# Every weight product of a two-layer encoder with the activation stationary, and the operands that TensorE turns for it

## The chip, the core and the metric

The kernel runs on one core of one Trainium2 chip. The metric is device time in microseconds (us), the median of the runs. The core has five engines that work side by side and wait for each other by semaphores: TensorE (PE; its loads of the stationary operand are listed as PEld), VectorE (DVE), ScalarE (ACT), GpSimd (POOL) and SyncE (SP), on whose queue all transfers are issued here.

## The reference

Two layers of an encoder over 256 tokens with 2048 features, all in float32: an input projection, eight attention heads beside a gated position-mixing branch, an output projection, and a gated feed-forward part.

```python
D_MODEL = 2048; SEQ = 256; DEPTH = 2; D_ATTN = D_GMLP = 1024; N_HEADS = 8; D_FF = 5632
...
    for l in range(DEPTH):
        h = rmsnorm(x, norm1_g[l])
        proj = jnp.einsum('bsd,de->bse', h, w_in[l])
        q = proj[..., 0:D_ATTN].reshape(B, S, N_HEADS, HEAD_DIM)
        k = proj[..., D_ATTN:2 * D_ATTN].reshape(B, S, N_HEADS, HEAD_DIM)
        v = proj[..., 2 * D_ATTN:3 * D_ATTN].reshape(B, S, N_HEADS, HEAD_DIM)
        uv = proj[..., 3 * D_ATTN:]
        q = apply_rope(q, cos, sin)
        k = apply_rope(k, cos, sin)
        a = dilated_attention(q, k, v)
        g = chunked_spatial_gating(uv, gmlp_ln_g[l], w_spatial[l], b_spatial[l])
        mix = jnp.concatenate([rmsnorm(a, mix_norm_attn_g[l]),
                               rmsnorm(g, mix_norm_gmlp_g[l])], axis=-1)
        x = x + jnp.einsum('bse,ed->bsd', mix, w_out[l])
        h = rmsnorm(x, norm2_g[l])
        ff = jax.nn.silu(jnp.einsum('bsd,df->bsf', h, w_gate[l])) * jnp.einsum('bsd,df->bsf', h, w_up[l])
        x = x + jnp.einsum('bsf,fd->bsd', ff, w_down[l])
    return rmsnorm(x, final_g)
```

The three windows of the attention lie within 256 tokens, so the kernel computes them as one attention with the logarithm of the count of patterns in its mask (`mskt`).

## The kernel before

Each float32 operand is written as the sum of a high part, rounded to the type that TensorE reads at full pace (float32r), and a low part; a product is made of three terms: high by high, high by low, low by high (`TERMS`). ACT writes the high part (`hi`, L731), DVE the low part (`lo`, L732). Weights are read once, in the order of their use, by loads of 1 MB on SP's queue (`raw`, four buffers); a load brings two chunks of [128, 1024], and each chunk is split into `hi` and `lo` (four buffers each). The loop over chunks (from L749) issues the load three loads ahead, the split three chunks ahead (`LA_SPLIT`), then the chunk's products, then at most two side tasks (`run_side`). This order is written out by the program, engine by engine, and each engine executes its own list in order.

A weight product has one of two forms. In the form "tok" (L776) the activation is stationary, [128 features, 128 tokens], and 512 weight columns stream: three matmuls of 512 columns for each k-tile (128 input features) and token tile. The result is [token, feature]. v, the gating branch and, in the last layer, the down projection have it. In the form "feat" (L784) a [128, 128] tile of the weights is stationary and the activation streams: the high part of the weights meets high and low part of the activation side by side (512 columns), the low part meets the high part (256 columns):

```python
                            ps[:, t, :SEQ if wl else 2 * SEQ], lhsT=wt[wl][:, j, t * P:(t + 1) * P],
                            rhs=a.t[:, ka, 0, :] if wl else a.t[:, ka].rearrange("p a t -> p (a t)"),
```

The result is [feature, token], which is the layout that the next product wants (`KTiles`: the activation as [feature, token], high and low part). q, k, w_out, gate, up and the down projection of layer 0 have it. The two halves of such a result (by the high and by the low part of the activation) are added at the eviction (`add_halves` L525, `Ffn.scaled` L536), and the norm's factor for each token is multiplied in from a row that is broadcast over partitions by a matmul (`to_row`, L220, from sums over features, L208). x is held as [feature, token] and turned to [token, feature] by TensorE once, before the last projection (`Ffn.turn`, L572), since the output is [token, feature] (`Final`).

Of the kernel before, what the change touches and what calls it, by code (L numbers as in the profile page):

```python
# [8 lines left out]
F32 = mybir.dt.float32  # L9
# [29 lines left out]
CH = 1024  # L39
KCH = {"tok": 2, "feat": 4}  # L40
LA_DMA = 3
LA_SPLIT = 3
START = 2
WARM = 4
TAIL = 3
TERMS = ((0, 0), (0, 1), (1, 0))
# w_in: (what, form, column, index); q and k by two heads, the others by halves
W_IN = tuple(
    [("v", "tok", 2 * DA + i * NB, i) for i in range(2)]
    + [(what, "feat", c + m * 2 * P, m) for m in range(NH // 2) for what, c in (("q", 0), ("k", DA))]  # L50
    + [("gv", "tok", 3 * DA + DG + i * NB, i) for i in range(2)]
    + [("u", "tok", 3 * DA + i * NB, i) for i in range(2)]
# [3 lines left out]
def _units():  # L56
    """The weight products in their order: (layer, weight, form, first row, k-tiles, first column, what, index)."""
    for l in range(DEPTH):
        for what, form, col, idx in W_IN:
            yield l, "w_in", form, 0, KD, col, what, idx  # L60
        for what, row, kt in (("oa", 0, NH), ("og", DA, NG)):
            for m in range(KD // 2):
                yield l, "w_out", "feat", row, kt, m * 2 * P, what, m
        j0 = 0
        for i, nj in enumerate(FF_PARTS):
            for m in range(2 * j0, 2 * (j0 + nj)):
                yield l, "w_gate", "feat", 0, KD, m * 2 * P, "gate", m
                yield l, "w_up", "feat", 0, KD, m * 2 * P, "up", m
            form, width = ("feat", 2 * P) if l + 1 < DEPTH else ("tok", NB)
            for m in range(D // width):  # L70
                yield l, "w_down", form, j0 * NB, nj * KR, m * width, f"down{i}", m
            j0 += nj
# [3 lines left out]
def encoder_kernel(ctx: ExitStack, tc: tile.TileContext, x, w, ws, lng, cols, fg, cs, msk, out):  # L76
# [36 lines left out]
    def load_x(k0, k1):  # L113
        b = k0 // KR
        nc.sync.dma_start(out=xt[b][:, k0 - b * KR:k1 - b * KR, :], in_=x[:, k0:k1, :])
# [747 lines left out]
```

## Time and profile before

| what | us |
|---|---|
| median of 3 runs | 2180.19 |
| lowest and highest | 2180.03 and 2181.32 |
| span of the profiled execution (first to last instruction) | 2178.5 |
| median less that span: what lies around the instructions | 1.7 |
| PE busy in the span | 2160.7 |
| DVE busy | 1431.8 |
| ACT busy | 981.7 |

The rows below come from the profiled execution and are measured against its span; the runs were timed apart. A busy PE is one with a matmul somewhere in its pipeline, so the pace of a kind of matmul is read from the distance of their starts, or from a long stretch with their number, and not from the duration of one. The granted clock of TensorE was at its full level in all 40 slices of the span.

### The profile page before, as it was taken

How to read it: one execution, taken by the hardware profiler on the slowest of the kernel's cores; microseconds unless marked ns; L12 is line 12 of the kernel's file. 1: busy time of each engine (PE TensorE's matmuls, PEld its weight loads, DVE VectorE, ACT ScalarE, POOL GpSimd, SP SyncE). 2: the span in 40 equal slices, each digit the busy share in tenths (PEclk: the TensorE clock that was granted, in tenths of full speed). 3: DMA queues.
4: the chain of work that ended last, by engine and by line, in shares of the span. 5: the costliest groups of instructions: out<-in, count | busy, mean ns of one | idle time of the engine just before them, and what ended most of it. 6: DMA issues, size and time to landing. Idle time of an engine off the chain costs nothing.

```text
span 2178.5 us, 28345 instructions
## 1 busy us (share of the span) xinstructions
PE 2160.7 (99%) x11692; PEld 1857.0 (85%) x11692; DVE 1431.8 (66%) x1515; ACT 981.7 (45%) x1192; POOL 120.4 (6%) x78
## 2 busy tenths in 40 slices
PE   8999999999999999999999999999999999999998
PEld 7888888888888888888888888888888888888886
DVE  6786677666556665566658866876665566645665
ACT  6455555443334443344545554554443344433443
POOL 2220002000000000000102200110000000000000
PEclk9999999999999999999999999999999999999999
DMA  7445555545554455554554455545455545555453
GB/s 289 167 155 193 181 187 186 182 175 200 186 193 179 176 201 179 193 186 177 199 187 162 156 191 183 184 176 192 185 184 193 186 180 193 193 193 193 180 207 116
DMA packets 57585, 404.01 MB, mean 185 GB/s; under 512 B 6512, under 2 KB 6512, under 8 KB 9456
## 3 DMA queue, kind: packets, MB, share of 16 engines
q1 hardware_dynamic: 57456, 402.21, 50.8%
q8 instruction: 91, 1.49, 0.3%
q14 instruction: 38, 0.31, 0.0%
HBM read 400.09 MB, written 2.10 MB: 185 GB/s over the span
## 4 chain that ended last, share of the span: by engine, by line
PE 94%; DVE 3%; ACT 2%; issue 0%; DMA 0%; SPq 0%; POOLq 0%; POOL 0%; DVEq 0%; ACTq 0%
PE mm L784 70%; PE mm L776 22%; ACT hi L731 1%; DVE lo L732 1%; DVE rb_k L339 1%; DVE rb_q L339 1%; ACT sm L386 0%; DVE pT L187 0%; PE op L409 0%; DVE mx L383 0%; PE mix L481 0%; DVE sm L378 0%; DMA raw<-in_w 0%; PE mm_end L776 0%; PE sp L373 0%
## 5 line engine op out<-in xcount | busy, mean ns | idle before, releaser
L732 DVE TENSOR_TENSOR lo<-raw,hi 128x1024 fp32r<-128x1024 f32 (+1 forms) x753 | 926.9, 1244 | 546.2 <-ACT hi L731 543.2
L784 PE MATMUL mm<-h_n,hi 128*128 128x512 f32 x3328 | 1165.6, 399 | 0.0
L731 ACT ACTIVATE hi<-raw 128x1024 fp32r<-128x1024 f32 (+1 forms) x753 | 784.2, 1054 | 626.2 <-PE mm L784 417.5
L784 PE MATMUL mm<-h_n,lo 128*128 128x256 f32 x3328 | 900.6, 281 | 0.0
L784 PEld LDWEIGHTS mm<-h_n,hi 128*128 128x128 f32 x3328 | 612.7, 188 | 133.6
L784 PEld LDWEIGHTS mm<-h_n,lo 128*128 128x128 f32 x3328 | 628.2, 189 | 20.0
L776 PE MATMUL mm<-hi,h_n 128*128 128x512 f32 x768 | 246.6, 396 | 4.6 <-ACT hi L731 4.6
L784 PE MATMUL mm<-ff,hi 128*128 128x512 f32 x704 | 245.0, 398 | 0.0
L776 PE MATMUL mm<-hi,ff 128*128 128x512 f32 x680 | 210.4, 389 | 0.0
L784 PE MATMUL mm<-ff,lo 128*128 128x256 f32 x704 | 189.8, 281 | 0.0
L776 PEld LDWEIGHTS mm<-hi,h_n 128*128 128x128 f32 x768 | 145.3, 189 | 34.9 <-ACT hi L731 4.9
L784 PEld LDWEIGHTS mm<-ff,hi 128*128 128x128 f32 x704 | 129.2, 188 | 27.9
L776 PE MATMUL mm<-lo,h_n 128*128 128x512 f32 x384 | 150.7, 392 | 0.0
L776 PEld LDWEIGHTS mm<-hi,ff 128*128 128x128 f32 x680 | 127.6, 188 | 26.5
L784 PEld LDWEIGHTS mm<-ff,lo 128*128 128x128 f32 x704 | 132.9, 189 | 4.7
L776 PE MATMUL mm<-lo,ff 128*128 128x512 f32 x340 | 132.3, 389 | 0.0
L179 ACT ACTIVATE ff<-up 128x512 fp32r<-128x512 f32 x44 | 27.8, 633 | 200.6 <-DVE up L553 200.6
L250 POOL TENSOR_TENSOR acc_n<-acc_n,sq_n 128x512 f32<-128x512 f32 x28 | 55.6, 1986 | 899.6 <-issue 688.4
L546 ACT ACTIVATE sil<-sil 128x512 f32<-128x512 f32 x44 | 27.9, 634 | 162.7 <-DVE sil L545 162.7
L525 DVE TENSOR_TENSOR xt<-mm,xt 128x512 f32<-128x512 f32 x112 | 77.4, 691 | 24.4 <-PE mm L784 21.9
L784 PE MATMUL mm<-a,hi 128*128 128x512 f32 x256 | 90.2, 402 | 0.0
L784 PE MATMUL mm<-g,hi 128*128 128x512 f32 x256 | 88.1, 397 | 0.0
(128 smaller groups left out, 1288.1 us busy)
## 6 DMA issues: line engine op xcount, KB each, us to landing
raw<-in_w SPq DMA_DIRECT2D x374, 1024.0 KB, 4.8
raw<-in_w SPq DMA_DIRECT2D x4, 512.0 KB, 7.4
out<-xn SPq DMA_DIRECT2D x8, 256.0 KB, 3.1
xt<-in_x SPq DMA_DIRECT2D x3, 512.0 KB, 8.3
ws<-in_ws SPq DMA_DIRECT2D x2, 512.0 KB, 5.7
lng<-in_lng SPq DMA_DIRECT2D x2, 512.0 KB, 6.5
fg<-in_fg SPq DMA_DIRECT2D x1, 1024.0 KB, 6.9
xt<-in_x SPq DMA_DIRECT2D x2, 256.0 KB, 4.4
```

Of the source, the lines that this page charges most:

```text
L179: nc.scalar.activation(out=hi, in_=src, func=AF.Copy)
L250: nc.gpsimd.tensor_tensor(out=self.acc, in0=self.acc, in1=sq, op=ALU.add)
L339: nc.vector.tensor_tensor(out=b[to], in0=s[of], in1=sin[of].to_broadcast([h, 2, SEQ]), op=ALU.mult)
L525: nc.vector.tensor_tensor(out=xb, in0=ps[:, :, i * SEQ:(i + 1) * SEQ], in1=xb, op=ALU.add)
L546: nc.scalar.activation(out=sil, in_=sil, func=AF.Silu)
L731: nc.scalar.activation(out=hi[:, sl], in_=src[:, sl], func=AF.Copy)
L732: nc.vector.tensor_tensor(out=lo[:, sl], in0=src[:, sl], in1=hi[:, sl].bitcast(F32), op=ALU.subtract)
L776: nc.tensor.matmul(bank[t][:, t], lhsT=a.part(hl, ka, t), rhs=wt[wl][:, j, :], start=(k == 0 and n == 0), stop=(k == kt - 1 and n == len(T ...
L784: nc.tensor.matmul(ps[:, t, :SEQ if wl else 2 * SEQ], lhsT=wt[wl][:, j, t * P:(t + 1) * P], rhs=a.t[:, ka, 0, :] if wl else a.t[:, ka].rea ...
```

## The change

All weight products take the form "tok": the program `_groups` replaces `_units`. A step is one load of 1 MB: two k-tiles by two blocks of 512 columns, for both token tiles, in one accumulator bank for each token tile and block (`mm`, five banks of 512 instead of two pairs of banks; three instead of four banks for the side work). Each of the two chunks of a step is now used for token tile 0 and again for token tile 1. Gate and up of the same 512 hidden features are one group, and so are q and k of four heads.

All results are [token, feature]; the norms' factors are scalars for each partition at the eviction, and the broadcast rows go. x stays as [token, feature]; the first layer's stationary operand comes from a second copy of x that is loaded as [feature, token] (`xf`). All other stationary operands are turned by TensorE, four transposes into one bank (`tpn` for the norms, `tpr` for q and k after the rotation, `tpf` for the hidden features), and split from there by ACT and DVE. The squares for the norms are summed along the free dimension by ACT.

```diff
+def _groups():
...
+            yield l, what, idx, 0, KD // 2, (("w_in", ca), ("w_in", cb))
...
+            for m in range(j0, j0 + nj):
+                yield l, "ff", m, 0, KD // 2, (("w_gate", m * NB), ("w_up", m * NB))
+            for m in range(2):
+                yield l, f"down{i}", m, j0 * NB, 2 * nj, (("w_down", 2 * m * NB), ("w_down", (2 * m + 1) * NB))
...
-    mmp = ctx.enter_context(tc.tile_pool(name="mm", bufs=2, space=PSUM))
-    sdp = ctx.enter_context(tc.tile_pool(name="sd", bufs=4, space=PSUM))
+    mmp = ctx.enter_context(tc.tile_pool(name="mm", bufs=5, space=PSUM))
+    sdp = ctx.enter_context(tc.tile_pool(name="sd", bufs=3, space=PSUM))
...
+        def block(self, b):
+            for k in (0, 2):
+                ps = transposes(xt[b], k, f"tpn_{self.which}_{self.l}_{b}_{k}")
+                yield 1
+                put_splits(self.blocks[b], k, ps, [gcol(self.l, self.which, b * KR + k + j) for j in range(2)])
+                yield 1
+            self.square(b)
...
+            ps = sdp.tile([P, 4, P], F32, tag="sd", name=f"tpr_{tag}")
+            for f in range(4):
+                nc.tensor.transpose(ps[:, f, :], a[:, f, :], ident)
...
+            self.silu = s2p.tile([P, NB], F32, tag="sx", name=f"sil_{self.l}_{m}_{t}", bufs=5)
+            nc.scalar.activation(out=self.silu, in_=ps, func=AF.Silu, scale=self.norm.scale(t))
...
+        def up(self, t, m, ps):
+            nc.vector.scalar_tensor_tensor(
+                out=self.ff[:, t, :], in0=ps, scalar=self.norm.scale(t), in1=self.silu, op0=ALU.mult, op1=ALU.mult
...
+            if t == NT - 1:
+                spawn(self.turn(m, self.ff), rank=0)
...
+        def turn(self, m, ff):
+            self.blocks[m] = KTiles(mpool, "mf", f"ff_{self.l}_{m}")
+            for k in (0, 2):
+                yield 1
+                ps = transposes(ff, k, f"tpf_{self.l}_{m}_{k}")
+                put_split2(self.blocks[m], k, ps.rearrange("p j t q -> p j (t q)"))
...
+        def block(self, b, t):
+            self.square(b, t)
+            xb = xt[b][:, t, :]
+            nc.vector.tensor_tensor(out=xb, in0=xb, in1=self.fg[:, b * NB:(b + 1) * NB], op=ALU.mult)
+            yield 0
...
+                elif b < D // NB - 1:
+                    if idx == 0:
+                        spawn(final.block(b, t), delay=2)
+                    else:
+                        for _ in final.block(b, t):
+                            pass
...
+    for b in range(D // NB):
+        nc.sync.dma_start(out=xt[b], in_=x[:, :, b * NB:(b + 1) * NB])
...
+    for i, (g, j) in enumerate(steps):
+        l, what, idx, _, pairs, _ = groups[g]
+        dma_to(i + LA_DMA)
+        split_to(2 * i + 1)
+        if j == 0:
...
-                    lo_first = k == kt - 1
-                    for wl in (1, 0) if lo_first else (0, 1):
+            banks = [[None, None] for _ in range(NT)]
+        hl = [hl_t.pop(2 * i + kk) for kk in range(2)]
+        acts = [lhs(l, what, 2 * j + kk) for kk in range(2)]
+        for t in range(NT):
+            state["slot"] = 2 * i + t
+            split_to(2 * i + t + min(LA_SPLIT, 1 + i))
+            for n in range(2):
+                if j == 0:
+                    banks[t][n] = mmp.tile([P, NB], F32, tag="mm", name=f"mm_{g}_{t}_{n}")
+                ps = banks[t][n]
+                for kk, (a, ka) in enumerate(acts):
+                    for z, (xl, wl) in enumerate(TERMS):
                         nc.tensor.matmul(
-                            ps[:, t, :SEQ if wl else 2 * SEQ], lhsT=wt[wl][:, j, t * P:(t + 1) * P],
-                            rhs=a.t[:, ka, 0, :] if wl else a.t[:, ka].rearrange("p a t -> p (a t)"),
-                            start=(k == 0 and wl == 0), stop=(lo_first and wl == 0),
+                            ps, lhsT=a.part(xl, ka, t), rhs=hl[kk][wl][:, n, :],
+                            start=(j == 0 and kk == 0 and z == 0),
+                            stop=(j == pairs - 1 and kk == 1 and z == len(TERMS) - 1),
                         )
-            if i + 1 == len(chunks):
-                done(l, what, idx, bank[t], (t,))
-        ready.clear()
-        if k0 + KCH[form] == kt and i + 1 < len(chunks):
-            done(l, what, idx, ps)
-        run_side()
+                if j == pairs - 1:
+                    done(l, what, idx, t, n, ps)
+            run_side()
```

What this does to the engines' lists is shown at three places. The first is PE in layer 0, in the first q product, where the second chunk of weights begins (before), and at the group's start (now); `h_n` is the normalised activation, `hi` and `lo` are the weights' parts, and the operand that streams stands first. Before:

```order
L784 MATMUL mm_511<-h_n_0_0_136,lo_440 128x256
L784 MATMUL mm_511<-h_n_0_0_136,hi_439 128x512
L784 MATMUL mm_511<-h_n_0_0_136,lo_440 128x256
L784 MATMUL mm_511<-h_n_0_1_170,hi_464 128x512
L784 MATMUL mm_511<-h_n_0_1_170,lo_465 128x256
L784 MATMUL mm_511<-h_n_0_1_170,hi_464 128x512
```

Now (the last three rows begin the second block, k, with the same stationary parts):

```order
L699 MATMUL mm_0_0_509<-hi_443,h_n_0_0_121 128x512
L699 MATMUL mm_0_0_509<-lo_444,h_n_0_0_121 128x512
L699 MATMUL mm_0_0_509<-hi_443,h_n_0_0_121 128x512
L699 MATMUL mm_0_0_509<-hi_461,h_n_0_0_121 128x512
L699 MATMUL mm_0_0_509<-lo_462,h_n_0_0_121 128x512
L699 MATMUL mm_0_0_509<-hi_461,h_n_0_0_121 128x512
L699 MATMUL mm_0_1_516<-hi_443,h_n_0_0_121 128x512
L699 MATMUL mm_0_1_516<-lo_444,h_n_0_0_121 128x512
L699 MATMUL mm_0_1_516<-hi_443,h_n_0_0_121 128x512
```

For 512 features, one k-tile and all tokens that is 6 products of 512 columns where there were 4 pairs of 512 and 256; the operands have changed places.

The second place is PE in layer 0's feed-forward part, behind the last product of the first 512 (before: 256) hidden features. Before, the next gate product follows at once:

```order
L784 MATMUL mm_3148<-h_n_0_3_3026,hi_3144 128x512
L784 MATMUL mm_3148<-h_n_0_3_3026,lo_3145 128x256 x2
L784 MATMUL mm_3148<-h_n_0_3_3026,hi_3144 128x512
L784 MATMUL mm_3240<-h_n_0_0_2711,hi_3165 128x512
L784 MATMUL mm_3240<-h_n_0_0_2711,lo_3166 128x256
L784 MATMUL mm_3240<-h_n_0_0_2711,hi_3165 128x512
```

Now two groups of transposes (`tpf`, from `ffn`, the hidden features as [token, feature]) stand among the products of the next block, one behind each token tile:

```order
L699 MATMUL mm_0_1_3134<-hi_3081,h_n_0_0_2454 128x512
L699 MATMUL mm_0_1_3134<-lo_3082,h_n_0_0_2454 128x512
L699 MATMUL mm_0_1_3134<-hi_3081,h_n_0_0_2454 128x512
L196 MATMUL tpf_0_0_3141<-ident,ffn_0_3091 128x128 x4
L699 MATMUL mm_1_0_3152<-hi_3063,h_n_0_0_2454 128x512
L699 MATMUL mm_1_0_3152<-lo_3064,h_n_0_0_2454 128x512
...
L699 MATMUL mm_1_1_3159<-hi_3081,h_n_0_0_2454 128x512
L196 MATMUL tpf_0_2_3166<-ident,ffn_0_3091 128x128 x4
L699 MATMUL mm_0_0_3127<-hi_3101,h_n_0_0_2454 128x512
```

The four transposes are added, and PE's list reaches the first of them 12 products behind the end of the block.

The third place is the end of DVE's list, from the last blocks of the last projection on (`xn` and `xt` are x as [token, feature], `r_f` the last norm's factor, `fg` its gain). Before, the last block alone stands at the end, token tile 0, then 1:

```order
L582 TENSOR_TENSOR xn_12315<-mm_17362,xn_12315 128x512
L618 TENSOR_SCALAR ms_f_17438<-ss_f,pre_f 128x1
L634 TENSOR_SCALAR xn_12075<-xn_12075,r_f_17440 128x512
L634 TENSOR_SCALAR xn_12233<-xn_12233,r_f_17440 128x512
L628 SCALAR_TENSOR_TENSOR xn_12315<-xn_12315,r_f_17440,fg 128x512
L582 TENSOR_TENSOR xn_12315<-mm_end,xn_12315 128x512
L618 TENSOR_SCALAR ms_f_17471<-ss_f,pre_f 128x1
L634 TENSOR_SCALAR xn_12075<-xn_12075,r_f_17473 128x512
L634 TENSOR_SCALAR xn_12233<-xn_12233,r_f_17473 128x512
L628 SCALAR_TENSOR_TENSOR xn_12315<-xn_12315,r_f_17473,fg 128x512
```

Now (token tile 0's last four rows and all of token tile 1):

```order
L548 TENSOR_SCALAR xt_109<-xt_109,r_f_15195 128x512
L548 TENSOR_SCALAR xt_111<-xt_111,r_f_15195 128x512
L542 SCALAR_TENSOR_TENSOR xt_112<-xt_112,r_f_15195,fg 128x512
L602 TENSOR_TENSOR xt_111<-mm_1_0_15023,xt_111 128x512
L519 TENSOR_TENSOR xt_111<-xt_111,fg 128x512
L602 TENSOR_TENSOR xt_112<-mm_1_1_15030,xt_112 128x512
L526 TENSOR_REDUCE tot_f_15222<-ss_f 128x1
L527 TENSOR_SCALAR pre_f<-tot_f_15222 128x1
L532 TENSOR_SCALAR ms_f_15227<-ss_f,pre_f 128x1
L548 TENSOR_SCALAR xt_109<-xt_109,r_f_15229 128x512
L548 TENSOR_SCALAR xt_111<-xt_111,r_f_15229 128x512
L542 SCALAR_TENSOR_TENSOR xt_112<-xt_112,r_f_15229,fg 128x512
```

Block 2 of token tile 1 (`xt_111`: add, then gain) has moved behind the scaling of token tile 0.

## Rows read from the trace of the kernel before

**Rows 1.** The page: busy time, share of the span, instructions of each engine.
```profile
PE 2160.7 (99%) x11692; PEld 1857.0 (85%) x11692; DVE 1431.8 (66%) x1515; ACT 981.7 (45%) x1192; POOL 120.4 (6%) x78
```

**Rows 2.** The page: shares of the chain that ended last, by engine.
```profile
PE 94%; DVE 3%; ACT 2%; issue 0%; DMA 0%; SPq 0%; POOLq 0%; POOL 0%; DVEq 0%; ACTq 0%
```

**Rows 3.** What PE waited for: us in total, times, longest.
```profile
PE mm L776 <- ACT hi L731: 4.6, 1, 4.6
...
PE op L409 <- DVE pT L187: 3.2, 6, 0.6
```

**Rows 4.** The chain in order of time, its long stretches: start, us, what.
```profile
202.22 27.25 PE mm L776 x120
...
358.79 734.19 PE mm L784 x4160
...
1613.58 87.05 PE mm L776 x384
...
1700.63 180.90 PE mm L784 x1024
```

**Rows 5.** Two stretches: length, busy time of PE, PEld, DVE, ACT, POOL; clock.
```profile
1613.58:1700.63 87.05, 87.05 (x386) 72.08 (x385) 45.95 (x42) 34.37 (x33) 0.00 (x0) 1.00 0.53 192
202.22:229.47 27.25, 27.25 (x122) 22.52 (x121) 21.19 (x26) 14.01 (x17) 1.60 (x1) 1.00 0.43 154
```

**Rows 6.** The chain's pieces near 170, 355 and 1455 us: start, us, what.
```profile
170.15 0.71 PE sp L373 x6
...
179.80 0.44 PE ptp L399 x4
...
180.24 2.76 PE mm L776 x12
...
355.08 0.34 PE ss_n L208 x4
...
358.36 0.43 PE row_n L220 x2
...
1454.82 0.44 PE tpx L572 x4
```

**Rows 7.** Timeline at a chunk's end in the last layer: start, us, instruction, idle before.
```profile
1624.08 0.62 PE L776 MATMUL mm<-hi,ff 128*128 128x512 f32 x2
...
1624.51 1.06 ACT L731 ACTIVATE hi<-raw 128x1024 fp32r<-128x1024 f32 x1 [1.61 <-PE mm L776]
```

**Rows 8.** Groups by form: instruction xcount, busy us, mean ns, idle before.
```profile
L731 ACT ACTIVATE hi<-raw 128x1024 fp32r<-128x1024 f32 x751 | 783.1, 1055 | 623.6 <-PE mm L784 417.5 <-PE mm L776 188.6 <-issue 5.7
...
L357 ACT ACTIVATE v<-mm,rstd_n 128x512 fp32r<-128x512 f32 x8 | 5.5, 683 | 5.1 <-PE mm L776 4.8 <-POOL rstd_n L201 0.3
...
L732 DVE TENSOR_TENSOR lo<-raw,hi 128x1024 fp32r<-128x1024 f32 x751 | 925.6, 1245 | 543.5 <-ACT hi L731 540.6
...
L358 DVE SCALAR_TENSOR_TENSOR v<-mm,rstd_n,v 128x512 fp32r<-128x512 f32 x8 | 6.0, 748 | 3.2 <-ACT v L357 3.2
```

**Rows 9.** Timeline of DVE, first and last instruction of one head's softmax.
```profile
93.08 0.69 DVE L378 SCALAR_TENSOR_TENSOR sm<-sp,mskt 128x512 f32<-128x512 f32 x1
...
95.86 0.62 DVE L392 TENSOR_SCALAR sm<-sm,rden 128x256 f32<-128x256 f32 x2
```

**Rows 10.** Timeline of the end.
```profile
2169.47 0.39 PE L776 MATMUL mm_end<-hi,ff 128*128 128x512 f32 x1
...
2169.89 0.69 DVE L582 TENSOR_TENSOR xn<-mm_end,xn 128x512 f32<-128x512 f32 x1
...
2173.11 0.75 DVE L628 SCALAR_TENSOR_TENSOR xn<-xn,r_f,fg 128x512 f32<-128x512 f32 x1
```

**Rows 11.** The chain's pieces from 2160 us.
```profile
2166.60 0.73 ACT junk_f L594 x2
```

**Rows 12.** The stretch from 24 to 28 us; last columns: DMA share, GB/s.
```profile
24.00:28.00 4.00, 4.00 (x19) 3.30 (x19) 4.00 (x5) 3.52 (x6) 3.26 (x2) 1.00 1.02 426
```

**Rows 13.** Timeline of ACT, the split that reads weight load 4.
```profile
24.51 1.06 ACT L731 ACTIVATE hi<-raw 128x1024 fp32r<-128x1024 f32 x1 [0.27 <-PE mm L776]
```

More of the change, by code (lines that the diff above doesn't have):

```diff
@@ L100, in encoder_kernel @@
     early = cpool.tile([P, 1], F32, name="early")
-    nc.scalar.activation(out=early, in_=ones[:, :1], func=AF.Copy)
+    nc.scalar.activation(out=early, in_=ones, func=AF.Copy)
     warm = sdp.tile([P, P], F32, tag="sd", name="warm")
@@ L262, in pair, with square @@
-        def pair(self, m):
-            self.square(m)
-            yield 1
-            self.put(m)
-            if self.n == KD // 2:
-                yield from self.finish()
-        def early(self, m, wait):
-            self.put(m)
-            yield wait
-            self.square(m)
-            if self.n == KD // 2:
-                yield 1
-                yield from self.finish()
+            self.rstd = None
+        def square(self, b):
+            for t in range(NT):
+                junk = s2p.tile([P, NB], F32, tag="junk", name=f"sq_{self.which}_{self.l}_{b}_{t}", bufs=1)
+                nc.scalar.activation(out=junk, in_=xt[b][:, t, :], func=AF.Square, accum_out=self.ss[:, t, b:b + 1])
+            self.n += 1
+            if self.n == D // NB:
+                tot = smp.tile([P, NT], F32, tag="tot", name=f"tot_{self.which}_{self.l}", bufs=2)
+                nc.vector.tensor_reduce(out=tot, in_=self.ss, axis=AX.X, op=ALU.add)
+                self.rstd = rstd_of(tot, D, f"{self.which}_{self.l}")
@@ new lines, in rope, with turn @@
+        def rope(self, name, m, t, ps):
+            l, tag = self.l, f"{name}_{self.l}_{m}_{t}"
+            s = s2p.tile([P, 4, HD], F32, tag="sx", name=f"s_{tag}", bufs=5)
+            nc.scalar.activation(out=s.rearrange("p h d -> p (h d)"), in_=ps, func=AF.Copy, scale=self.norm.scale(t))
+            spawn(self.turn(name, m, t, s), rank=0)
+        def turn(self, name, m, t, s):
+            tag = f"{name}_{self.l}_{m}_{t}"
+            a = s2p.tile([P, 4, HD], F32, tag="sx", name=f"ra_{tag}", bufs=5)
+            b = s2p.tile([P, 4, HD], F32, tag="sx", name=f"rb_{tag}", bufs=5)
@@ L527, in encoder_kernel, with lhs, scale @@
+        def lhs(self, what, k):
+            of = self.a if what == "oa" else self.g
+            force(lambda: of[k // KR] is not None and of[k // KR].ready[k % KR])
+            return of[k // KR], k % KR
+        def scale(self, what, t):
+            force(lambda: (self.ra if what == "oa" else self.rg) is not None)
+            return (self.ra if what == "oa" else self.rg)[:, t:t + 1]
     class Ffn:
@@ L703, in encoder_kernel @@
-    units = list(_units())
-    chunks = [(u, k) for u, un in enumerate(units) for k in range(0, un[4], KCH[un[2]])]
+            mixers[l].gate_u(t, n, ps)
+        elif what == "ff":
+            (ffns[l].up if n else ffns[l].gate)(t, idx, ps)
+        else:
+            b = 2 * idx + n
+            xb = xt[b][:, t, :]
+            if what in ("oa", "og"):
+                nc.vector.scalar_tensor_tensor(
+                    out=xb, in0=ps, scalar=mixers[l].scale(what, t), in1=xb, op0=ALU.mult, op1=ALU.add
+                )
+            else:
+                nc.vector.tensor_tensor(out=xb, in0=ps, in1=xb, op=ALU.add)
+            if what == "og" and t == NT - 1:
+                spawn(norms["n2", l].block(b), delay=1 + 4 * n)
+            if what == last_part:
+                if l + 1 < DEPTH:
+                    if t == NT - 1:
+                        spawn(norms["n1", l + 1].block(b), delay=1 + 4 * n)
+                elif b < D // NB - 1:
+                    if idx == 0:
+                        spawn(final.block(b, t), delay=2)
+                    else:
+                        for _ in final.block(b, t):
+                            pass
+                else:
+                    final.last(t)
@@ L705, in encoder_kernel @@
+    groups = list(_groups())
+    steps = [(g, j) for g, gr in enumerate(groups) for j in range(gr[4])]
     raw_t, hl_t = {}, {}
```

489 lines of the change are left out of this document (162 added, 327 removed).

## The prediction

> **What bounds the kernel now.** I read the page first. TensorE (PE) is busy for 99% of the span, and the chain that ended last runs over PE for 94% of it [rows 1, 2]. The waits by engine say how little PE stands still: the largest wait in the middle of the run is 3.2 us in total, the other one is the wait for the first weights [rows 3]. So the time is the sum of what PE is given to do, plus a start and a tail, and VectorE (DVE) and ScalarE (ACT) count only where PE would wait for them. Which weight products are dear is read from the chain in order of time, since its pieces run from one start to the next and leave out the overlap that is inside the recorded durations [rows 4].
>
> **The products.** A chunk of 1024 weight columns carries 6144 streamed columns in either form: 12 products of 512, or 8 pairs of 512 + 256. The weights-stationary form (L784) took 734.19 us for 4160 matmuls, 0.1765 us each, so 16 x 0.1765 = 2.824 us for a chunk; the stretch at 1700.63 gives 2.827. The activation-stationary form (L776) took 87.05 us for 384, 0.2267 each, 2.720 us for a chunk, and 2.725 in the stretch at 202.22 [rows 4]. So the form that has four matmuls fewer costs 0.1035 us less for the same columns. That is not a matter of the traffic beside it: L776 ran at the same pace with DVE busy 53% of the stretch and with 78% [rows 5]. From the shapes, the chunks in the old form are q and k 32, w_out 32, gate and up 176 in each layer, and the down projection of layer 0, 88: 568. The gain is 568 x 0.1035 = **58.8 us**.
>
> At this place the Trainium skill speaks against the change. Its page "TensorE: Matmul & The Clock Gate" (section "Back-to-back issue gap") lets a matmul take its columns / 2.4 GHz + 2.5 ns, nearly in proportion to the columns: 2.590 us for a chunk in the new form and 2.600 in the old one, by which the gain would be an estimated 6 us and the time, with all else as below, an estimated 2216. The rows say 2.720 and 2.824.
>
> **New work on PE.** Activations that come out as [token, feature] must be turned before they can be stationary: for each later norm 8 groups of four transposes (3 x 8), for q and k 16 groups over both layers, for the hidden features 2 in each of 22 blocks: 24 + 16 + 44 = 84 groups. The groups that are there now cost 0.44 us each on the chain, among products of either form, and the chunk behind one took 2.76 instead of 2.72 [rows 6]. I take 0.46: 84 x 0.46 = **+38.6 us** (bounds 0.44 and 0.48: 37 to 40). Fallen away: 8 groups that turned x before the last projection, 8 x 0.46 = 3.7; four sums over features at 0.34 and six row broadcasts at 0.43 [rows 6], 3.9: **-7.6 us**. All other matmuls (scores, probabilities, mixing) keep their number and shape.
>
> **Work on DVE and ACT.** The wide evictions with a broadcast row go, smaller ones with a scalar for each token come; PE hides both, as DVE was busy 66% and ACT 45% [rows 1]. What matters is where PE can now be late, and there are four places.
>
> (1) Turning the hidden features. Let T be the end of the last product of a gate/up block. Before that, ACT was handed the split of a later chunk, whose buffer is that of the first chunk of this step. Both token tiles read it now, the last time 3 products before T, at T - 0.68. A split starts about 0.2 us after the last product that reads its buffer: the product pair that starts at 1624.08 ends a chunk at 1624.31, the split starts at 1624.51 [rows 7]. So it runs from T - 0.48 to T + 0.58 (1.055), silu behind it to T + 1.26 (0.683, by the nearest eviction that scales from PSUM), the low part on DVE from T + 0.65 to T + 1.9 (1.245), and the product with silu to T + 2.65 (0.748) [rows 8]. PE reaches the transposes that need it one slot after T, at T + 2.72. There is no slack. The same holds where the last blocks of w_out and of the down projection become the next norm's input, 6 times. 28 places at 0 to 0.3 us: I take 0.1, **+2.8 us** (0 to 8.4).
>
> (2) The attention heads. A head's softmax holds DVE for 3.4 us, from 93.08 to 96.48 [rows 9], as its in-order queue waits for the exponentials. Behind it stands the low part of the second chunk of the step after next. In a step without a head that is done at about T + 3.1 and wanted at T + 5.44 + 0.68: 3 us of slack, where the old order split three chunks of 2.7 to 2.8 us ahead and had about 8.2 - 1.1 - 1.2 = 5.9. With a head it ends near T + 6.8, and the scores have put off the need by 0.71 [rows 6] to T + 6.8. So slack is zero again in 16 places; where evictions through gelu fall beside heads some tenths are missing. 0 to 0.6 us each, taken as **+2.0 us** in all (0 to 10); the row for PE waiting on probabilities, 3.2 us now [rows 3], says that such waits stay small.
>
> (3) The tail. Now the last block of token tile 0 is finished while tile 1 is still being multiplied; one chain of add, square, scale takes 3.97 us from 2169.89 to 2173.11 + 0.75, and ends 4.16 us behind the last product's end (2169.47 + 0.23) [rows 10]. In the new order each token tile brings two blocks of 512 at the very end, on one DVE queue. For block 2: add 0.69, square with its read 0.73 [rows 11], scaling 0.69, with the hand-overs 2.3 us; then 3.97 for block 3. Tile 0's block 2 is complete 18 products before T, so its add starts at T - 3.9: 2.3 and 3.97 bring tile 0 to T + 2.4, and tile 1's two blocks, queued behind it, end at T + 8.7. That is **+4.5 us** (0 if DVE work were hidden, 6 at most).
>
> (4) The start. 2.1 MB more (x in both layouts) go through the queue ahead of weight load 4, and the engines were moving 426 GB/s then [rows 12], so this load lands up to 4.9 us later. Now its split starts at 24.51 and waits for PE, not for the load [rows 13]; 4.9 us later it starts by 29.4, and the products want it about 8 chunks after the clock came up, near 32. The second half of it is late by under 1 us, since two splits of activations stand between. The first weights come in quarters, so PE starts earlier and then waits. Taken as **+1.0 us** (-1 to +3).
>
> **Sum.** 2178.5 - 58.8 + 38.6 - 7.6 + 2.8 + 2.0 + 4.5 + 1.0 = 2161.0 us span. The median of the runs shown lies 1.7 us above the profiled span, so **2162.7 us**, 0.8% less. With the bounds of all terms at one end: 2149 to 2182.
>
> **Rivals.**
> - *PE never waits for the new work*: terms 1 and 2 are zero, and the tail is hidden. For it: in a block without heads only one eviction stands between. 2161.0 - 2.8 - 2.0 - 4.5 + 1.7 = 2153.
> - *The turn waits each time*: PE stands 0.6 us at each of the 28 places, as DVE's queue brings the product with silu one hand-over later and PE also loses the early weight load. +14 us: 2177, no change that a measurement can tell (about 0.2%, 4.4 us, is what can be told here). For it: slack is zero by the rows; against it: the row of PE waiting for probabilities has 0.6 us as its longest wait, and these fell on 6 of 16 heads.
> - *The split is late in the attention stretches*, ends slower: both chunks of a step are now held to the end of the step, with the same four buffers, so that the queues have 3 us less room. In q, k and the two halves of the gating there are 4 groups x 8 steps x 2 layers = 64 steps. If PE loses 0.6 us in each, that is 38 us, 36 more than I took: 2199. It decides from 17.5 / 64 = 0.27 us a step on. Against it: a head comes only every 2 to 4 slots, and PE lost 3.2 us in all there so far.
> - *The columns alone set the cost*: the old form's extra 0.1 us a chunk would then belong to something that stays. No gain, all of the new work: 2161.0 + 58.8 + 1.7 = 2221. Against it stand four stretches of two forms [rows 4], which differ by form and by nothing else that I find. The rule of the Trainium skill's TensorE page above comes near to this one.
>
> **How the numbers follow.** Forecast 0.73 (own range 2155 to 2172), no waits 0.09, turn waits 0.10, late splits 0.06, columns alone 0.02. The range 2153 to 2177 leaves out half of the no-wait case, almost half of the turn case and the two slow ones, 0.17 together. Faster by over 0.2% (below 2175.8): 0.73 + 0.09 + 0.02 of the turn case = 0.84; within 0.2%: 0.08, the turn case; slower 0.08, the two slow cases.
>
> **What would show it.** In the profile after, PE's products in one form only, 9024 of them at 0.2267 us on the chain; groups of four transposes at 0.44; PE's wait list led by transposes or products waiting for DVE, under 10 us in all; DVE less busy; the last eviction some 8.7 us behind the last product. The forecast is wrong if the pace of the products differs from 0.2267, if a transpose group in the new places costs over 0.6 with its wait, or if PE's share of the span falls below 98%.

## The result and the profile after

The changed kernel takes 2168.14 us (median of 4 runs, 2167.43 to 2170.74), the one before 2180.28 (4 runs): ratio 0.9947, 95% interval 0.9933 to 0.9961, 12.1 us less. The forecast was 2162.7 in a range of 2153 to 2177, so the gain came 5.4 us short of it. The profiled execution is the longest of the four, 2170.74 us with a span of 2168.9; the spans of the others were 2165.6 to 2166.6.

The page, busy time of each engine (it answers to [rows 1]):
```profile
PE 2138.9 (99%) x9696; PEld 1770.0 (82%) x9696; DVE 1169.3 (54%) x1258; ACT 958.1 (44%) x1215; POOL 85.8 (4%) x64
```
PE is still the bound, and DVE has fallen from 66% to 54%. The chain in order of time, long stretches and one block's turn (start, us, what; as [rows 4] and [rows 6]):
```profile
402.26 2.76 PE mm L699 x12
405.02 0.44 PE tpf L196 x4
405.46 40.84 PE mm L699 x180
...
538.86 127.88 PE mm L699 x564
```
One form is left, at 127.88 / 564 = 0.2267 us a product, and a group of four transposes costs 0.44 with 2.76 for the 12 products behind it. Both are as forecast. What PE waited for (total, times, longest; as [rows 3]):
```profile
PE mm L699 <- DVE lo L647: 7.8, 8, 1.3
PE mm L699 <- ACT hi L646: 5.0, 2, 4.4
PE mm L699 <- ACT s_q L293: 2.9, 2, 1.5
```
No transposes stand in this list: the turn of the hidden features and of x holds PE up nowhere. Products wait instead for the low part of a weight chunk and for the eviction of q. Where that is, PE's timeline says; these are the rows that end idle time in layer 0's second q/k block (idle before in brackets):
```profile
166.28 0.50 PE L699 MATMUL mm<-lo,h_n 128*128 128x512 f32 x1 [0.66 <-DVE lo L647]
...
168.50 0.71 PE L699 MATMUL mm<-lo,h_n 128*128 128x512 f32 x1 [1.26 <-DVE lo L647]
169.01 1.05 PE L699 MATMUL mm<-hi,h_n 128*128 128x512 f32 x2
```
At 169.01 the products are slower as well. Two stretches of 5 us (length; busy time of PE, PEld, DVE, ACT, POOL; granted clock, DMA share, GB/s) show why:
```profile
165.00:170.00 5.00, 3.07 (x10) 1.89 (x9) 4.53 (x6) 0.66 (x2) 2.13 (x1) 0.86 0.11 13
170.00:175.00 5.00, 5.00 (x22) 3.95 (x21) 3.39 (x4) 2.89 (x4) 0.00 (x0) 0.80 0.66 223
```
Behind idle time the granted clock stood at its lower level, 1.2 GHz, for 5 x (0.14 + 0.20) / 0.5 = 3.4 us. Read from one product's start to the next, less 0.2267 us a product, the gaps of layer 0 are 1.45 us at 113.6 (end of the first q/k block), 1.61 at 155.5, 0.83 at 165.0 and 1.44 at 166.6 (end of the second), and 1.7 for the lower clock; layer 1 has the same four places again, 5.3 us. That is 12.3 us at four block ends. DVE and POOL there:
```profile
151.96 2.95 DVE L305 TENSOR_TENSOR rb_q<-s_q,cst 128x256 f32<-128x256 f32 x2
155.04 1.84 DVE L305 TENSOR_TENSOR rb_k<-s_k,cst 128x256 f32<-128x256 f32 x2
156.80 1.21 DVE L647 TENSOR_TENSOR lo<-raw,hi 128x1024 fp32r<-128x1024 f32 x1
...
160.18 2.95 DVE L305 TENSOR_TENSOR rb_q<-s_q,cst 128x256 f32<-128x256 f32 x2
163.23 1.85 DVE L305 TENSOR_TENSOR rb_k<-s_k,cst 128x256 f32<-128x256 f32 x2
165.01 3.44 DVE L647 TENSOR_TENSOR lo<-raw,hi 128x1024 fp32r<-128x1024 f32 x2
```
```profile
159.25 2.16 POOL L302 TENSOR_TENSOR ra_q<-s_q,cst 128x512 f32<-128x512 f32 x1
161.37 1.47 POOL L302 TENSOR_TENSOR ra_k<-s_k,cst 128x512 f32<-128x512 f32 x1
163.27 1.53 POOL L307 TENSOR_TENSOR ra_q<-ra_q,rb_q 128x512 f32<-128x512 f32 x1 [0.43 <-DVE rb_q L305]
165.23 2.13 POOL L307 TENSOR_TENSOR ra_k<-ra_k,rb_k 128x512 f32<-128x512 f32 x1 [0.43 <-DVE rb_k L305]
```
The new order finishes q and k of both token tiles in one step, so four rotations come in a row, each with POOL and DVE at once. In the kernel before they lay apart; two pieces of its chain, and POOL's timeline at the start of a rotation of q and of the next, of k:
```profile
144.72 0.69 DVE rb_q L339
145.42 1.68 DVE rb_q L339
```
```profile
144.83 1.73 POOL L336 TENSOR_TENSOR ra_q<-s_q,csr 128x512 f32<-128x512 f32 x1 [7.38 <-DVE s_q L322]
160.76 1.74 POOL L336 TENSOR_TENSOR ra_k<-s_k,csr 128x512 f32<-128x512 f32 x1 [12.22 <-DVE s_k L322]
```
In the changed kernel a DVE product with sin for q (128x256) takes 1.48 us on average beside POOL, and two low parts take 3.44 instead of 2.4. The two low parts from 165.01 are what PE waits for at 166.28 and 168.50.

At the end DVE works in a row (timeline, as [rows 10]; the last product starts at 2155.61, so T is 2155.84):
```profile
2157.92 0.68 DVE L602 TENSOR_TENSOR xt<-mm,xt 128x512 f32<-128x512 f32 x1
2159.45 0.69 DVE L519 TENSOR_TENSOR xt<-xt,fg 128x512 f32<-128x512 f32 x1 [0.85 <-ACT junk_f L513]
2160.05 0.68 DVE L602 TENSOR_TENSOR xt<-mm,xt 128x512 f32<-128x512 f32 x1
...
2163.26 0.75 DVE L542 SCALAR_TENSOR_TENSOR xt<-xt,r_f,fg 128x512 f32<-128x512 f32 x1
```
The last eviction ends at 2164.01, T + 8.2, against T + 4.16 before and T + 8.7 in the forecast.

### The profile page after: what moved, and what is told of

It reads as the page before. It is cut to its first block, busy times and chain, and to the rows that moved or that the text cites. A ratio compares the mean times of both kernels' runs of the same rounds, so it can differ in the third digit from the quotient of the medians.

```text
span 2168.9 us, 24017 instructions
## 1 busy us (share of the span) xinstructions
PE 2138.9 (99%) x9696; PEld 1770.0 (82%) x9696; DVE 1169.3 (54%) x1258; ACT 958.1 (44%) x1215; POOL 85.8 (4%) x64
## 4 chain that ended last, share of the span: by engine, by line
PE 95%; DVE 2%; DMA 1%; issue 0%; ACT 0%; SPq 0%; POOL 0%; POOLq 0%; DVEq 0%; ACTq 0%
PE mm L699 92%; DVE lo L647 1%; PE tpf L196 1%; DVE rb_q L305 1%; DMA raw<-in_w 1%; PE sp L333 1%; PE op L367 1%; PE tpn_n L196 0%; DMA xf<-in_xf 0%; PE ptp L359 0%; PE mix L436 0%; DVE rb_k L305 0%; ACT hi L646 0%; PE tpg L196 0%; SPq L666 0%
## 5 line engine op out<-in xcount | busy, mean ns | idle before, releaser
L699 PE MATMUL mm<-hi,h_n 128*128 128x512 f32 x4096 | 1291.1, 392 | 7.9 <-ACT hi L646 5.0
L699 PEld LDWEIGHTS mm<-hi,h_n 128*128 128x128 f32 x4096 | 771.0, 188 | 167.6 <-ACT hi L646 6.2
L699 PE MATMUL mm<-lo,h_n 128*128 128x512 f32 x2048 | 800.7, 391 | 7.8 <-DVE lo L647 7.8
L699 PEld LDWEIGHTS mm<-lo,h_n 128*128 128x128 f32 x2048 | 385.8, 188 | 89.1 <-DVE lo L647 12.6
L699 PE MATMUL mm<-hi,ff 128*128 128x512 f32 x1408 | 438.9, 390 | 0.0
L699 PEld LDWEIGHTS mm<-hi,ff 128*128 128x128 f32 x1408 | 264.3, 188 | 54.6
L699 PE MATMUL mm<-lo,ff 128*128 128x512 f32 x704 | 274.0, 389 | 0.0
L699 PEld LDWEIGHTS mm<-lo,ff 128*128 128x128 f32 x704 | 132.2, 188 | 27.0
L699 PE MATMUL mm<-hi,a 128*128 128x512 f32 x256 | 84.1, 399 | 0.0
L699 PE MATMUL mm<-hi,g 128*128 128x512 f32 x256 | 81.3, 392 | 0.0
```

The lines of the kernel that those rows point to most:

```text
L699: nc.tensor.matmul(ps, lhsT=a.part(xl, ka, t), rhs=hl[kk][wl][:, n, :], start=(j == 0 and kk == 0 and z == 0), stop=(j == pairs - 1 and kk ...
```

## Experiments

Each edit is made to the changed kernel, and medians are compared with its 2168.1 us; the kernel before ran beside them at 2179.7 to 2180.1. The first question is what the block ends of q and k wait for.

**Rotation on DVE alone.**
```diff
-            nc.gpsimd.tensor_tensor(out=a, in0=s, in1=cos, op=ALU.mult)
+            nc.vector.tensor_tensor(out=a, in0=s, in1=cos, op=ALU.mult)
-            nc.gpsimd.tensor_tensor(out=a, in0=a, in1=b, op=ALU.add)
+            nc.vector.tensor_tensor(out=a, in0=a, in1=b, op=ALU.add)
```


> Edit: the product with cos and the sum in the rotation of q and k run on DVE instead of POOL. In the changed kernel PE loses 12.4 us at the ends of the four q/k blocks (gaps of 0.8 to 1.6 us at 113.6, 155.5, 165.0, 166.6, 1187.0, 1229.0, 1238.5, 1240.1, and 1.7 us of lower clock from 168.5). Theory A (two engines at once slow each other): the products with sin take 1.48 us while POOL works on the same tiles, against 0.42 us for the same shape elsewhere; without POOL they take 0.42, a q or k tile takes DVE 2.2 us (2 x 0.42 + 2 x 0.69) instead of up to 2.95, ACT waits less for the rotation buffers, and PE's loss falls to 4 to 7 us: 2161 to 2165. Theory B (DVE's queue is simply full there): 22 us more work for DVE in just these stretches makes PE lose more: 2169 to 2178.

2157.03 us (2156.88 to 2157.18), ratio to before 0.9895 (0.9881 to 0.9908): 11.1 us less, more than theory A gave. DVE does POOL's work too and is finished sooner. Its groups by form (busy us, mean ns):
```profile
L305 DVE TENSOR_TENSOR rb_q<-s_q,cst 128x256 f32<-128x256 f32 x16 | 6.0, 419 | 0.1
L302 DVE TENSOR_TENSOR ra_q<-s_q,cst 128x512 f32<-128x512 f32 x8 | 5.5, 684 | 0.0
L307 DVE TENSOR_TENSOR ra_q<-ra_q,rb_q 128x512 f32<-128x512 f32 x8 | 5.5, 684 | 0.0
```
In the changed kernel the first of these groups alone had more than all three together have here (17.0):
```profile
L305 DVE TENSOR_TENSOR rb_q<-s_q,cst 128x256 f32<-128x256 f32 x16 | 23.0, 1476 | 0.4 <-PE tpr_q L314 0.4
```
PE's waits for the low part are 0.9 us instead of 7.8 (of which 6.4 lay at the ends of q/k blocks), and the wait for q's eviction is gone:
```profile
PE mm L699 <- DVE lo L647: 0.9, 3, 0.3
```
Theory B falls. The run takes away what DVE and POOL cost each other and the hand-overs between them (0.43 us each in POOL's rows above) together; how the 11.1 us divide is not shown.

**POOL at work on a tile that DVE does not touch.**
```diff
+                if self.l == 1:
+                    c = cst.rearrange("p a t d -> p (a t d)")
+                    nc.gpsimd.tensor_tensor(out=c, in0=c, in1=c, op=ALU.mult)
```


> Edit: in layer 1's 22 gate/up blocks POOL multiplies a tile by itself (128 x 512, the rope constants, no longer read by then) twice a block, 44 operations that nothing waits for. It asks whether it is POOL's work as such, on a tile that DVE does not touch, that slows DVE. Theory (the two engines slow each other): DVE operations that fall beside a POOL operation take longer, as the low part beside the rotation (3.44 us for two, 1.72 each, against 1.23), and POOL's operation takes 1.5 to 2.2 us; DVE's busy time in these blocks rises by some 0.4 to 1 us for each POOL operation, 18 to 44 us in all, and PE, which has slack there, loses little. Rival (it was the common tile of the rotation, or the queue, that stretched DVE's operations): the low parts stay at 1.23 us and DVE's busy time does not change.

The counts in the expectation are wrong: a layer has 11 such blocks, so there were 22 operations. Nothing ordered them, and they ran back to back from 1453. POOL's timeline, then DVE's during and after (idle before in brackets):
```profile
1453.00 34.87 POOL L499 TENSOR_TENSOR cst<-cst 128x512 f32<-128x512 f32 x22
```
```profile
1454.29 3.93 DVE L650 TENSOR_TENSOR lo<-raw,hi 128x1024 fp32r<-128x1024 f32 x2 [2.02 <-ACT hi L649]
...
1472.52 0.74 DVE L485 SCALAR_TENSOR_TENSOR ffn<-mm,rstd_n,sil 128x512 f32<-128x512 f32 x1
...
1488.43 2.36 DVE L650 TENSOR_TENSOR lo<-raw,hi 128x1024 fp32r<-128x1024 f32 x2 [1.46 <-ACT hi L649]
```
Two low parts take 3.2 to 4.0 us while POOL works and 2.36 after it, though they share no tile with it. The product with silu, one of whose inputs lies in PSUM, keeps its 0.74. Single instructions of the same timelines say how the time is lost:
```profile
1454.12 1.04 POOL L499 TENSOR_TENSOR cst<-cst 128x512 f32<-128x512 f32 x1
1454.29 1.95 DVE L650 TENSOR_TENSOR lo<-raw,hi 128x1024 fp32r<-128x1024 f32 x1 [2.02 <-ACT hi L649]
1455.24 1.90 POOL L499 TENSOR_TENSOR cst<-cst 128x512 f32<-128x512 f32 x1
1456.16 2.06 DVE L650 TENSOR_TENSOR lo<-raw,hi 128x1024 fp32r<-128x1024 f32 x1
```
The low part of 1454.29 ends at 1456.24, 1.08 us after POOL's operation has ended (1455.16). POOL's next one ends 0.90 after that low part, and the second low part 1.08 after this one. So here the two take turns: each of these instructions waits until the other engine's has ended, and then takes about its own time. The rotation shows the same: POOL's sum of 165.23 ends at 167.36, the second low part from 165.01 at 168.45. The Trainium skill's page "SBUF — State Buffer" (section "Who interferes with whom") has this rule: a DVE instruction with two SBUF inputs contends with a GpSimd (POOL) instruction that reads SBUF, one with at most one SBUF input, outside DVE's 2-port modes, does not. These rows agree, the low part having two (raw and hi). Over layer 1's feed-forward stretch the low parts cost 323.9 us instead of 316.9: 7.0 / 22 = 0.32 us for each POOL operation, in a stretch where DVE is idle half the time. That is less than the 0.4 to 1 expected. The one run took 2170.35 us, within the range of the changed kernel; PE had the slack.

**The split one chunk further ahead.**
```diff
-LA_DMA = 3
-LA_SPLIT = 3
+LA_DMA = 2
+LA_SPLIT = 4
```
Raw buffers 4 to 3, high and low parts 4 to 5.

> Edit: five buffers instead of four for the high and the low parts of weight chunks, the split one chunk further ahead; weight loads get three buffers instead of four to make room. Theory (PE's 12.4 us at the ends of the q/k blocks are lateness of the split that one more chunk, 2.72 us, can cover): the gaps that wait for the low part (0.8 to 1.45 us) vanish, the two of 1.6 us that wait for q's eviction stay or shrink, 2158 to 2162. Rival (the queues of DVE and ACT are in order, and a chunk further ahead stands behind the same evictions): less than 2 us gained, 2166 to 2168. Rival 2 (three load buffers are too few): PE or ACT waits for weights, slower than 2170.

2160.00 us (2159.73 to 2160.79), ratio 0.9908 (0.9895 to 0.9922): 8.1 us less. The waits for the low part fall from 7.8 to 0.6 us, those for q's eviction stay:
```profile
PE mm L699 <- ACT s_q L293: 2.9, 2, 1.5
...
PE mm L699 <- DVE lo L647: 0.6, 2, 0.4
```
So most of the lateness is covered by 2.72 us more of slack, even with POOL as it was.

**More buffers for the rotation** (5 to 8, raw buffers 4 to 3, loads issued two ahead instead of three).
```diff
-name=f"s_{tag}", bufs=5
+name=f"s_{tag}", bufs=8
```


> Edit: eight buffers instead of five for the tiles of the rotation of q and k (and silu), three weight load buffers instead of four to make room. Theory (ACT's eviction of the second q tile waits 3.75 us for a buffer that the first rotation still holds, PE waits 1.6 us for that eviction twice, and the splits behind it on ACT come late): the two gaps of 1.6 us vanish and those at 165 and 1238 shrink: 2162 to 2165. Rival (the buffer only moves the wait, since DVE then still works through the same products with sin): at most 1 us less, 2167 to 2168.

2165.76 us (2165.22 to 2167.18), ratio 0.9935 (0.9922 to 0.9947), 2.4 less, between the theory's 2165 and the rival's 2167. The wait for q's eviction is gone, but a part comes back further on, as k's transposes now wait for POOL:
```profile
PE mm L699 <- DVE lo L647: 5.7, 8, 1.3
...
PE tpr_k L314 <- POOL ra_k L307: 2.6, 2, 1.3
```

The second question is whether the two large terms of the sum were right.

**Gate and up in the old form.**
```diff
+                        for f in (2 * t, 2 * t + 1):
+                            fs = slice(f * P, (f + 1) * P)
...
+                            nc.tensor.matmul(ps, lhsT=hl[kk][0][:, n, fs], rhs=a.t[:, ka].rearrange("p h q -> p (h q)"),
...
+                            nc.tensor.matmul(ps[:, :SEQ], lhsT=hl[kk][1][:, n, fs], rhs=a.t[:, ka, 0, :],
```


> The gate and up products alone go back to the old form, weights stationary, 512 + 256 streamed columns; they are summed into the same four banks as now, so the output is another, but evictions, splits, buffers and loads are those of the changed kernel. Theory (the pair form costs 0.1035 us a chunk more for the same columns): 352 chunks x 0.1035 = 36.4 us more, 2204.5. Rival (columns alone set the cost, the old kernel's extra belonged to the work around it): no change, 2168. By the rule of the Trainium skill's page on TensorE's matmul and clock (section on the back-to-back gap), 2.5 ns a matmul, it would be an estimated 352 x 4 x 0.0025 = 3.5 us more.

2204.66 us (2202.78 to 2206.12): 36.5 more, against 36.4 from the term. PE's timeline at 700 us; a pair takes 700.38 - 700.03 = 0.35 us:
```profile
700.03 0.40 PE L703 MATMUL mm<-h_n,hi 128*128 128x512 f32 x1
700.26 0.28 PE L705 MATMUL mm<-h_n,lo 128*128 128x256 f32 x1
700.38 0.40 PE L703 MATMUL mm<-h_n,hi 128*128 128x512 f32 x1
```

**Twice as many matmuls for the same columns.**
```diff
+                        for c in (slice(0, 256), slice(256, 512)):
...
+                                ps[:, c], lhsT=a.part(xl, ka, t), rhs=hl[kk][wl][:, n, c],
```


> Edit: each product of 512 columns becomes two of 256, with the same stationary operand loaded for each; all else stays. It asks where the 0.1035 us a chunk come from. Theory (each matmul costs a fixed time beyond its columns): a 512-column product takes 0.2267 us, 13 ns over 512 columns at 2.4 GHz (0.2133); 9024 matmuls more x 13 ns = 121 us more, about 2289. By the share of the 256-column matmul in the old form (0.1172 us on the chain) it would be 9024 x (2 x 0.1172 - 0.2267) = 70 us, 2238. Rival (columns alone): 2168. By the rule of the Trainium skill's page on TensorE's matmul and clock (back-to-back gap), 2.5 ns a matmul, an estimated 22 us more.

2277.08 us (one run), 109 more. The chain:
```profile
559.27 135.36 PE mm L700 x1128
```
A product of 256 columns takes 135.36 / 1128 = 0.1200 us, one of 512 0.2267. From the two: 0.1067 us for 256 columns, and 0.0133 for the matmul itself. By the rows 9024 x 0.0133 = 120 us, 11 more than the time shows; PE's waits for the low part and for q's eviction are 5.1 us shorter here (3.8 and 1.8), and there is no dip of the clock in the middle, as in five of seven profiles with the changed kernel's waits; the rest of the 11 stays open. So matmuls cost by their number, each with its load of the stationary operand, which this edit doubles as well: of the 0.1035 us a chunk, four matmuls are 0.053. The other 0.050 stays open; the old form's matmuls, 16 in 2.824 us, are 3 ns dearer each than this rule makes them, perhaps by the alternation of two widths, which was not tried. The 2.5 ns of the Trainium skill's page "TensorE: Matmul & The Clock Gate" (section "Back-to-back issue gap") is not what these rows show; 13.3 ns is. The section gives the 2.5 ns for a matmul by itself and says that in a stream with loads of the stationary operand both set the pace, so it was not the rule for these products.

**No turn of the hidden features** (44 groups of transposes left out, the split reads the unturned tile).
```diff
-                ps = transposes(ff, k, f"tpf_{self.l}_{m}_{k}")
```


> Leaves out the 44 groups of transposes that turn the hidden features of gate/up; the split reads the unturned tile instead, so the output is another. Theory (a group of four costs PE 0.44 us on the chain and nothing waits for it): 44 x 0.44 = 19.4 us less, 2148.7. Rival (each place also has a wait that the wait list does not show, 0.6 us and more): 26 us or more less, 2142 or below.

2147.03 us (2146.49 to 2147.63), 21.1 less: 0.48 us a group, which is the 0.44 on the chain and the 0.04 by which the 12 products behind a group are longer. No wait hides there.

The third is the start and the tail.

**First load whole; x in token layout later.**
```diff
-                for c in range(4):
-                    nc.sync.dma_start(out=t[:, c], in_=w[r, :, c])
+            nc.sync.dma_start(out=t, in_=w[r])
```


> Edit: the first weight load comes as one transfer of 1 MB again, not as four quarters; the rest of the changed kernel stays. Theory (the quarters cost the start): in the profile of the changed kernel the products of the first 8 us run in fits, PE stands 0.57 us at 10.35, and the granted clock is at its lower level until 15.05, against 13.1 before; summed over the first 15 us the products lose 4.3 us to the lower clock and to gaps, against 2.5 us before. With one load the clock rises near 13.1 and the time falls by 1.8 us, from 2168.1 to about 2166.3. Rival (the quarters bring the first product forward and that is worth as much): no change, 2168.1 within 0.5.

```diff
+        if i in (2, 3):
+            for b in range(2 * i - 4, 2 * i - 2):
+                nc.sync.dma_start(out=xt[b], in_=x[:, :, b * NB:(b + 1) * NB])
```


> Edit: the 2 MB of x in token layout, the rope constants and the mask are issued behind weight loads 5 and 6, not ahead of load 4; the sums of squares that read x start two slots later. Theory (load 4 is late by the bytes ahead of it): PE's gaps at 33.71 (0.65 us) and 35.14 (1.14 us) go away, 1.8 us less, about 2166.3. Rival 1 (those gaps belong to ACT's order of work, not to the load): 2168.1. Rival 2 (x now comes too late for the row scale that the first eviction needs): PE waits at the end of step 8 and the time rises by 1 to 4 us.

First load whole: 2167.64 us (2167.19 to 2168.29), the rival's answer: the first product starts at 9.58 instead of 7.83, and the 17th at 16.04 against 15.76, one profile each. The theory falls. x later: 2166.79 (2166.70 to 2167.52), 1.3 of the 1.8 expected, 0.8 if each is set against the kernel before that ran beside it. Load 4 was late by the bytes ahead of it: its split on ACT waited for the load until 32.44 and now starts at 27.51 without such a wait. The gaps at 33.7 and 35.1 are gone too, but they do not prove it: of the seven profiles of kernels that begin with the same instructions, x in its old place, three have 1.4 to 1.8 us there and four have 0 to 0.4, 0.8 on average.

**The tail, three ways.** In the last step, block by block instead of tile by tile:
```diff
+        if i == len(steps) - 1:
+            order = [(t, n) for n in range(2) for t in range(NT)]
```


> Edit: in the last step alone the four banks are finished block by block (block 2 of both token tiles, then block 3 of both) instead of tile by tile. Theory (the tail grew because each tile brings two blocks at the end, on one DVE queue): the last eviction ends about 4.2 us behind the last product instead of 8.2, so the time falls by 4 us to about 2164.1. Rival (DVE's work in the tail is the same in sum, so the order matters little; or what follows the last eviction, the write to memory, is the bound): at most 1 us less, 2167 to 2168.

2167.77 us (2167.25 to 2169.95), no gain; the rival was right. DVE's timeline, with T at 2153.37:
```profile
2149.49 0.69 DVE L602 TENSOR_TENSOR xt<-mm,xt 128x512 f32<-128x512 f32 x1 [4.03 <-PE mm L702]
2150.97 0.69 DVE L519 TENSOR_TENSOR xt<-xt,fg 128x512 f32<-128x512 f32 x1 [0.79 <-ACT junk_f L513]
2151.58 0.68 DVE L602 TENSOR_TENSOR xt<-mm,xt 128x512 f32<-128x512 f32 x1
...
2160.80 0.74 DVE L542 SCALAR_TENSOR_TENSOR xt<-xt,r_f,fg 128x512 f32<-128x512 f32 x1
```
It ends at T + 8.2 again. Each block 2 holds DVE's queue for 2.1 us (0.8 of it in wait for ACT's square, since the gain overwrites what that reads) and each block 3 for 3.9: 12 us in a row from T - 3.9 in either order. Fewer passes and fewer waits were then tried (one scaling of tile 1 moves to ACT as well), with the rotation on DVE, x later and a reordered start:
```diff
+                elif n == 0:
+                    final.square(b, t)
+                    if t == 1:
+                        final.rstd(0)
+                        final.finish(0, (1,))
...
+                        final.finish(0, (0, 2))
+                        final.rstd(1)
+                        final.finish(0, (3,))
+                        final.finish(1, (1, 2, 0, 3))
```


> Edit: the rotation's product with cos and sum on DVE (as in the run before), x in token layout behind weight loads 5 and 6, and two new ones. Start: the first step takes the quarters of the weight load in the order in which they arrive, and the second half of the first x block is loaded behind them. Tail: block 2 is not multiplied by the final gain in a pass of its own but in the last scaling, and the last additions of tile 1 are queued on DVE ahead of the scaling of tile 0. Theory: rotation 2157.0; the loads 1.3 less as measured; start 0.6 to 1.2 less, since PE's gap of 0.57 at 10.35 closes and the clock rises before 14; tail: the last eviction ends 4.6 to 5.2 us behind the last product instead of 8.2, 3.0 to 3.6 less. Together 2151 to 2152. Rival (the tail is not shortened by fewer passes, as it was not by another order): 2154.5 to 2155.5.

2155.09 us (2153.30 to 2156.51), ratio 0.9890 (0.9873 to 0.9906), short of the 2151 to 2152. The tail did what was said; the start did not, and the runs lie further apart, for a cause that stays open. In the profile PE has new gaps of 1.5 us in all at 15.9 and 17.1. Hence the last run, without the edits of the start (x later among them):

> Edit: the rotation on DVE and the tail with fewer passes, without the edits of the start. The run with all of them gave a last eviction 4.8 us behind the last product, 3.4 us less than 8.2, and yet a median only 1.9 us below the rotation alone. Theory (the edits of the start gain nothing, since the spread of the first transfers covers them, and the tail's gain is whole): 2157.0 - 3.4 = 2153.6. Rival 1 (the start edits helped, and the tail gives back part of its 3.4 us in the writes to memory): 2155.5 to 2157. Rival 2 (the start edits cost time): 2152 or below.

2153.73 us (2153.60 to 2153.84), ratio 0.9879 (0.9863 to 0.9896): the theory's 2153.6. DVE's last rows, with T at 2142.20:
```profile
2142.40 0.69 DVE L610 TENSOR_TENSOR xt<-mm,xt 128x512 f32<-128x512 f32 x1 [0.55 <-PE mm L713]
...
2145.62 1.42 DVE L550 SCALAR_TENSOR_TENSOR xt<-xt,r_f,fg 128x512 f32<-128x512 f32 x2 [0.45 <-POOL r_f L541]
```
It ends at T + 4.8. This is the fastest version found, 14.4 us below the change as it was made.

## Why the prediction was right, and where it was off

Its sum against the two profiled executions (spans 2178.5 and 2168.9, 9.6 us less; forecast 17.5):

| step | forecast | measured |
|---|---|---|
| products, new transposes, work removed | -27.8 | -26.2 (what the other rows leave of -9.6) |
| (1) turn waits | +2.8 | 0 (none in the wait list) |
| (2) attention | +2.0 | +9.1 (12.3 less the 3.2 of [rows 3], which are gone) |
| (3) tail | +4.5 | +4.0, and 0.2 behind the last eviction |
| (4) start | +1.0 | +3.3: 1.5 to the 17th product (15.76 against 14.29), 1.8 by load 4 |

The medians differ by 12.1 us and not by 9.6: some 2.5 us of the right column belong to the profiled execution, the longest of its four. Some luck kept the sum in its range, as errors of both signs met: the waits of (1), 2.8 us, did not come.

- **Products**: right in size and mechanism by the old form put back (36.5 for 36.4), and the rival that columns alone set the cost is refuted by it and by the halves.
- **Transposes**: 0.48 each by the run without them, my upper bound; 0.46 was taken, 84 x 0.02 = 1.7 us too little, about the difference in the first line, which is itself a remainder.
- **(1)** Slack of zero turned out enough: the run without the turn shows no hidden wait.
- **(2)** is the step that failed: mechanism right, place and size wrong. I looked for lateness of the split at the 16 heads. The place was the end of the four q/k blocks, where the change makes four rotations due in one step (5.44 us) instead of lying apart; they keep POOL at work from 151.50 to 167.36. The sum has no term for them. The price, 12.3 us, was in two things that I did not read: POOL's share of the rotation, and how DVE waits for it. The waits for DVE and for q's eviction, 10.7 us, passed the "under 10 us in all" that the prediction named. The trace of before has the cause too: its product with sin took 0.69 to 1.69 us. The rule of the Trainium skill's page "SBUF — State Buffer" quoted above would have pointed there. The rival of late splits had the mechanism too, spread thinly over 64 steps; its 38 us did not come, as the steps without a rotation lost nothing. Without POOL 11.1 us come back; one more chunk of slack hides 8.1 of the lateness without touching its cause.
- **(3)** The chain of DVE passes was summed rightly, 8.7 for 8.2.
- **(4)** The split of load 4 started at 32.44, not "by 29.4", and PE lost 1.8 us there in this execution, more than the "under 1 us"; in the seven profiles with the same start it lost 0 to 1.8. The rest of the start is chance to a good part too: in those seven the 17th product came anywhere from 14.3 to 16.2 us. The section on the time before has the clock at its full level in all 40 slices; in the first one it was not: until 13.0 us before, and 15.0 after, the products come 0.43 us apart (the pace of the lower level) or more, and then 0.23.

The 1.7 us of the lower clock count in (2). They belong to this execution: of the other kernels with the same waits, the one with POOL's extra work shows the dip too, while those with another first load, later x, another tail, no turn, or gate and up in the old form do not. Without them (2) is +7.4.

## What to carry to other kernels

Where TensorE is the bound, count matmuls and not columns alone: fewer, wider products with the same columns gain the fixed part of each one. When a change moves evictions together, list what every engine does at that place, POOL too, and price DVE's operations on two SBUF tiles by how they ran beside POOL, not alone. The tail on DVE's in-order queue got 3.4 us shorter by fewer passes, fewer waits and one scaling on ACT together; another order of the same passes gained nothing.

## What was not expected of the hardware

- DVE and POOL take turns, one instruction at a time, without sharing a tile, where DVE reads two SBUF tiles: two low parts 3.2 to 4.0 us against 2.36, a 128x256 product 1.48 against 0.42, POOL's 128x512 product of the constants 1.90 against 1.04. Moving POOL's share to DVE made DVE's own time in the q/k stretch smaller (100 to 175 us: 56.3 busy instead of 58.3).
- A matmul of this type (fp32r, 128x128 stationary, a new one each time) costs 13.3 ns beyond its columns at 2.4 GHz; in pairs of 512 and 256 columns it is some 3 ns more.
- The time at which the granted clock rises at the start differed by 3.3 us between kernels that begin with the same instructions (12.8 us with another tail, 16.2 in the last run), and a dip behind idle time in the middle came in two of seven profiles with the same waits.
